# A hybrid attention and convolution block: gate and up computed by tokens, their product turned by VectorE and a trip through DRAM

## Chip, core and metric

The kernel runs on one core of one Trainium2 chip (trn2). The metric is the device time of one execution in microseconds, the median of three timed runs. The engines are named PE (TensorE matmul), PEld (TensorE weight load), DVE (VectorE), ACT (ScalarE), POOL (GpSimd) and SP (SyncE, which here only issues DMAs).

## What is computed

One block over 256 tokens of width 1024: a normalized input is projected, half of the width goes through attention with 8 heads, half through a causal convolution of 31 taps, both are projected back and added to the residual. Then comes the part that the change touches, a gated feed-forward layer of inner width 2816, and a last normalization:

```
h = h + mixed @ w_out[l]
u = rms_norm(h, ffn_norm_g[l])
h = h + (jax.nn.silu(u @ w_gate[l]) * (u @ w_up[l])) @ w_down[l]
...
return rms_norm(h, final_norm_g)
```

All inputs are float32.

## The kernel before

Every float32 operand of a large product is split into a high part (rounded to the fast float32r type, by ACT) and a low part (the rest, by DVE), and each product is three matmuls: high by high, high by low, low by high. The weights come in by SP's DMAs as raw tiles of 128 x 1024 (`load`, six buffers), `high` and `split` (L130 to L154) make `wh` and `wl` of them (nine buffers each), and `cut` (L156) takes columns out of them. Activations are kept turned, with the model width on the partitions: `xs` is the residual, `u2` holds the high and the low half of the normalized input, `uh` and `ul`, for all 256 tokens.

The phases ahead of the feed-forward layer follow a list of steps written out by hand (PROGRAM, L41). Its last lines hold the output projection (`f`), the lower halves of u (`g`), the squares for the norm (`hs`) and the first splits of the gate and up weights (`w.g0.0` and so on). Up to the product of group 0 all engines keep program order; then, at L627, ACT, DVE, POOL and SP are handed to the scheduler of the framework, and only PE stays in program order.

The feed-forward layer runs over 11 groups (FG) of 256 inner columns. For a group, `gate_up` (L552) has the weights as the held operand, 128 inner columns at a time (i), and streams u: one pass of 512 columns for the high weights (`uh` and `ul` side by side) and one of 256 for the low weights with `uh`, for 8 k, for gate and up (j). Gate and up come out with the inner width on the partitions, each in a PSUM bank of its own, four banks a group out of four. Group 0 goes by k in passes of 256 (`up_mm`, L548). `swiglu` (L572) adds the two halves of a bank (`both`: a copy on ACT, an addition on DVE), multiplies the gate by the per-token scale `rb2` (a broadcast that PE makes as `pb_h`, L616), takes Silu on ACT, multiplies by up on DVE and splits the product `ff` into `fh` and `fl`. These already have the form in which `down` (L588) holds them: 128 tokens by 128 inner rows, with `w_down` streamed in passes of 512, 24 passes a group, into four PSUM banks `pd` that are summed over all groups. On PE the order is gate-and-up of group g+1, then down of group g; the last two groups (HOLD, L620) are held back for the end. `h_rows` (L602) turns the residual for the end on PE, four transposes in each of the groups 1 to 4, into `ht`. At the end each half of the tokens gets its last products, the residual is added, squares are summed, and the scaled rows go out (L641 to L679).

Of the kernel before, what the change touches and what calls it, by code (L numbers as in the profile page):

```python
# [15 lines left out]
P = 128  # L16
S = 256
# [31 lines left out]
pv.0 mo.0 pv.1 mo.1 l.6 pv.2 mo.2 pv.3 mo.3 l.3 w.o1.1 ld.g0 w.o2.0 w.o2.1 ld.u0 o.0 o.1 l.7 w.o3.0 o.2 w.o3.1 ld.g1 l.4 l.5 w.g0.0 o.3 w.u0.0 o.4  # L49
f.0 f.1 g.0 f.2 g.1 f.3 g.2 f.4 g.3 f.5 g.4 f.6 g.5 f.7 g.6 g.7 w.g0.1 ld.u1 w.u0.1 ld.d0 hs.0 hs.1 hs.2 hs.3 hs.4 hs.5 hs.6 hs.7 w.g1.0 w.g1.1  # L50
# [9 lines left out]
def block_kernel(ctx, tc, xT, w_in, w_out, w_gate, w_up, w_down, pvec, gfin, relb, hot, out):  # L60
# [29 lines left out]

    steps = [t.split(".") for t in PROGRAM.split()]
# [452 lines left out]
    rb2 = w2.tile([P, S], F32, name="rb2")  # L544
    pd = [[bank(2 * t + n, f"pd{t}{n}") for n in range(2)] for t in range(2)]
    pf, acts = {}, {}

    def up_mm(g, i, j, k, start):  # L548
        mm3(pf[g][i][:, j * S : (j + 1) * S], "gu"[j] + str(g), k * S + i * P,
            uh[:, k], ul[:, k], start, k == KD - 1)  # L550

    def gate_up(g):  # L552
        pf[g] = []
        for i in range(2):
            pf[g].append([bank(next(spare), f"pf{2 * g + i}{j}") for j in range(2)])
            for j in range(2):
                o = pf[g][i][j]
                for k in range(KD):
                    wh, wl = cut("gu"[j] + str(g), k * S + i * P, P)
                    if k < KD - 1:  # L560
                        mm(o, wh, u2[:, k], start=k == 0, stop=False, skip_group_check=True)
                    mm(o[:, 0:S], wl, uh[:, k], start=False, stop=False, skip_group_check=True)
                    if k == KD - 1:
                        mm(o, wh, u2[:, k], start=False, stop=True, skip_group_check=True)

    def both(o, name):
        t = w2.tile([P, S], F32, name=name, tag="fb", bufs=2)
        act.copy(t, o[:, S : 2 * S])  # L568
        vec.tensor_add(t, o[:, 0:S], t)  # L569
        return t  # L570

    def swiglu(g):  # L572
        acts[g] = []
        for i in range(2):
            f = 2 * g + i
            gr = w2.tile([P, S], F32, name=f"fg{f}", tag="fg", bufs=2)
            vec.tensor_mul(gr, both(pf[g][i][0], f"fa{f}") if g else pf[g][i][:, 0:S], rb2)
            sg = w2.tile([P, S], F32, name=f"fs{f}", tag="fs", bufs=2)
            act.activation(sg, gr, AF.Silu)
            ff = w2.tile([P, S], F32, name=f"ff{f}", tag="ff", bufs=2)  # L580
            vec.tensor_mul(ff, sg, both(pf[g][i][1], f"fb{f}") if g else pf[g][i][:, S : 2 * S])
            fh = w2.tile([P, S], F32R, name=f"fh{f}", tag="fh", bufs=8)
            act.copy(fh, ff)
            fl = w2.tile([P, S], F32R, name=f"fl{f}", tag="fl", bufs=8)
            vec.tensor_sub(fl, ff, fh.bitcast(F32))  # L585
            acts[g].append((fh, fl))

    def down(g, i, t, lo, hi, o=None, start=None, stop=None):  # L588
        f = 2 * g + i
        tok = slice(t * P, (t + 1) * P)  # L590
        wh, wl = cut(f"d{g}", i * D + lo, hi - lo)
        fh, fl = (a[:, tok] for a in acts[g][i])
        if o is None:
            o = pd[t][lo // 512][:, lo % 512 : lo % 512 + hi - lo]
            start, stop = f == 0, f == NF - 1
# [12 lines left out]
    pf[0] = [bank(next(spare), f"pf{i}") for i in range(2)]  # L608
    for k in range(KD):
        for i in range(2):  # L610
            for j in range(2):
                up_mm(0, i, j, k, k == 0 and j == 0)
        if k == 5:
            rc2, dg2 = rstd(acch, D, RMS_EPS, "h", next(spare))
# [5 lines left out]
    HOLD = 2  # L620
    for g in range(FG):
        if 0 < g < FG - 1:
            split(f"g{g + 1}")
            split(f"u{g + 1}")
        swiglu(g)
        if g == 0:
            act, vec, pool, sync = nc.scalar, nc.vector, nc.gpsimd, nc.sync  # L627
        split(f"d{g}")
        if g + 1 < FG:
            gate_up(g + 1)  # L630
        if g < FG - HOLD:
            for i in range(2):
                for t in range(2):
                    for n in range(2):
                        down(g, i, t, n * 512, n * 512 + 512)
        if 1 <= g <= 4:
            h_rows((g - 1) // 2, (g - 1) % 2)


    held = [(g, i) for g in range(FG - HOLD, FG) for i in range(2)]  # L640
    for t in range(2):  # L641
# [8 lines left out]
        def square_rows(i, lo, hi):  # L650
            sq = w2.tile([P, 512], F32, name=f"fsq{t}{i}", tag="fsq", bufs=2)
            act.activation(sq[:, : hi - lo], ht[:, t, lo:hi], AF.Square, accum_out=ss[:, i : i + 1])
            vec.tensor_mul(hg[:, lo:hi], ht[:, t, lo:hi], gf[:, lo:hi])
# [9 lines left out]
        pe = bank(next(spare), f"pe{t}")  # L663
        for n, (g, i) in enumerate(held):
            down(g, i, t, 768, 1024, pe[:, 0:S], n == 0, n == len(held) - 1)
        ms = w2.tile([P, 2], F32, name=f"fms{t}")
        vec.tensor_add(ms[:, 0:1], ss[:, 0:1], ss[:, 1:2])
        vec.tensor_scalar(ms[:, 0:1], ms[:, 0:1], 1.0 / D, RMS_EPS, op0=ALU.mult, op1=ALU.add)
        add_rows(pe[:, 0:S], 768, 1024)
        square_rows(2, 768, 1024)  # L670
        vec.scalar_tensor_tensor(ms[:, 1:2], ss[:, 2:3], 1.0 / D, ms[:, 0:1], op0=ALU.mult, op1=ALU.add)
        rf = w2.tile([P, 1], F32, name=f"rf{t}")
        pool.tensor_tensor(rf, ms[:, 1:2], mhalf[:, 0:1], op=ALU.pow)
        vec.tensor_scalar(hg[:, 0:384], hg[:, 0:384], rf, None, op0=ALU.mult)
        nc.sync.dma_start(out[rows, 0:384], hg[:, 0:384])
        act.activation(hg[:, 384:704], hg[:, 384:704], AF.Copy, scale=rf)
        nc.scalar.dma_start(out[rows, 384:704], hg[:, 384:704])
        vec.tensor_scalar(hg[:, 704:1024], hg[:, 704:1024], rf, None, op0=ALU.mult)
        nc.sync.dma_start(out[rows, 704:1024], hg[:, 704:1024])  # L679
# [30 lines left out]

def _layout(x, mix_norm_g, w_in, rel_bias, conv_w, conv_b, conv_ln_g, conv_ln_b, w_out,
            ffn_norm_g, w_gate, w_up, w_down, final_norm_g):
    flat = lambda a: np.ascontiguousarray(a.reshape(P, -1))
    wi = _rows(w_in[0])
# [9 lines left out]
    pairs = lambda w: flat(_rows(w).reshape(P, KD, FG, S).transpose(0, 2, 1, 3))  # L724
# [33 lines left out]
```

## Time and profile before

| | |
|---|---|
| timed runs | 303.37, 303.93, 304.09 us; median 303.93 us |
| profiled execution | 304.98 us, of which the span from the first to the last instruction is 303.2 us |
| PE | 294.6 us busy, 1984 matmuls |
| DVE | 218.4 us busy |
| ACT | 166.6 us busy |
| DMA | 56.39 MB, mean 186 GB/s |
| feed-forward layer | from 109.4 us to the end |

The profile is of one execution. Busy time of PE is that of pipelined matmuls whose ends are modelled, so distances between the starts of matmuls say more than their durations. The chain of waits follows the work that ended last back to the start; a piece in it names the engine, the tile and the line.

### The profile page before, as it was taken

The page shows a single profiled execution, that of the slowest core. Times are in us where ns is not written, and L with a number is a line of the kernel's source. Part 1 is how long each engine was busy: PE and PEld are TensorE (multiplying, and loading weights), DVE is VectorE, ACT ScalarE, POOL GpSimd, SP SyncE. Part 2 cuts the span into 40 slices and gives each one's busy share as a digit, 9 for nine tenths or more (in the row PEclk, how much of TensorE's full clock was granted, in tenths as well). Part 3 has the DMA queues.
Part 4 walks back from the last instruction along what each step waited for, and adds up shares of the span by engine and source line. Part 5 has one row for each costly group of instructions (what it writes and reads, how often), then busy time and mean ns, then how long its engine had stood idle before and what let it go on. Part 6 is the DMA issues. An engine that isn't in the chain of part 4 may idle for free.

```text
span 303.2 us, 5198 instructions
## 1 busy us (share of the span) xinstructions
PE 294.6 (97%) x1984; PEld 258.6 (85%) x1984; DVE 218.4 (72%) x405; ACT 166.6 (55%) x300; POOL 8.2 (3%) x27
## 2 busy tenths in 40 slices
PE   8999999999999999999999999999999999999991
PEld 8998987897699999878888888888888888888891
DVE  3877999888987788898665749485665748383483
ACT  3875554364583678674645636374645546371242
POOL 4000000000000000000000000000000000000000
PEclk9999999999999999999999999999999999999998
DMA  6999879744418426988583846648283837300012
GB/s 186 351 387 325 260 181 287 312 138 142 128 23 301 142 105 200 298 283 282 189 271 83 273 136 216 199 129 272 83 277 85 277 129 240 109 0 2 0 54 85
DMA packets 18936, 56.39 MB, mean 186 GB/s; under 512 B 2221, under 2 KB 5061, under 8 KB 18912
## 3 DMA queue, kind: packets, MB, share of 16 engines
q1 hardware_dynamic: 18176, 54.99, 56.4%
q0 software_dynamic: 304, 0.74, 0.9%
q8 instruction: 15, 0.25, 0.3%
q10 hardware_dynamic: 432, 0.34, 0.3%
q14 instruction: 9, 0.07, 0.1%
HBM read 54.41 MB, written 1.65 MB: 185 GB/s over the span
## 4 chain that ended last, share of the span: by engine, by line
PE 74%; issue 11%; DMA 6%; DVE 3%; ACT 3%; SPq 1%; POOL 1%; POOLq 0%; DVEq 0%
PE pf L72 34%; PE pd L72 17%; PE pqk L72 7%; DMA raw_a<-in_w_in 4%; PE pv L72 4%; PE pc L72 4%; PE py L72 2%; DMA raw_u<-in_w_up 2%; PE ps L72 1%; SPq L83 1%; ACT wh_a L83 1%; PE pa L72 1%; PE pg L72 1%; PE pt L75 1%; PE po L72 1%
## 5 line engine op out<-in xcount | busy, mean ns | idle before, releaser
L72 PE MATMUL pf<-u,wh_u 128*128 128x512 f32 (+1 forms) x192 | 64.1, 375 | 0.6 <-DVE ff L83 0.6
L72 PE MATMUL pf<-u,wh_g 128*128 128x512 f32 (+1 forms) x192 | 64.6, 377 | 0.0
L72 PE MATMUL pf<-u,wl_g 128*128 128x256 f32 x176 | 46.1, 281 | 0.0
L72 PE MATMUL pf<-u,wl_u 128*128 128x256 f32 x176 | 46.1, 281 | 0.0
L72 PEld LDWEIGHTS pf<-u,wh_u 128*128 128x128 f32 x192 | 34.9, 188 | 6.0 <-DVE ff L83 0.9
L72 PEld LDWEIGHTS pf<-u,wh_g 128*128 128x128 f32 x192 | 34.9, 188 | 5.3
L72 PEld LDWEIGHTS pf<-u,wl_u 128*128 128x128 f32 x176 | 33.1, 188 | 1.7
L72 PEld LDWEIGHTS pf<-u,wl_g 128*128 128x128 f32 x176 | 33.2, 188 | 1.5
L154 DVE TENSOR_TENSOR wl_u<-raw_u,wh_u 128x1024 fp32r<-128x1024 f32 x18 | 21.9, 1224 | 16.7 <-ACT wh_u L144 16.7
L72 PE MATMUL pd<-wh_d,fh 128*128 128x512 f32 (+1 forms) x88 | 33.7, 383 | 0.0
L72 PE MATMUL pd<-wh_d,fl 128*128 128x512 f32 (+1 forms) x88 | 33.5, 381 | 0.0
L72 PE MATMUL pd<-wl_d,fh 128*128 128x512 f32 (+1 forms) x88 | 33.4, 379 | 0.0
L144 ACT CAST wh_u<-raw_u 128x1024 fp32r<-128x1024 f32 x18 | 18.9, 1048 | 17.9 <-PE pd L72 9.6
L154 DVE TENSOR_TENSOR wl_d<-raw_d,wh_d 128x1024 fp32r<-128x1024 f32 x22 | 26.8, 1216 | 0.7 <-ACT wh_d L144 0.6
L154 DVE TENSOR_TENSOR wl_g<-raw_g,wh_g 128x1024 fp32r<-128x1024 f32 x18 | 22.0, 1223 | 4.7 <-ACT wh_g L144 4.3
L144 ACT CAST wh_g<-raw_g 128x1024 fp32r<-128x1024 f32 x18 | 18.9, 1050 | 9.0 <-PE pd L72 7.9
L144 ACT CAST wh_d<-raw_d 128x1024 fp32r<-128x1024 f32 x22 | 22.7, 1052 | 1.4 <-PE pd L72 1.1
L72 PE MATMUL pqk<-u,wh_qk 128*128 128x256 f32 x128 | 23.1, 282 | 0.0
L569 DVE TENSOR_TENSOR fb<-pf,fb 128x256 f32<-128x256 f32 x20 | 8.4, 419 | 19.1 <-ACT fb L568 19.1
L72 PEld LDWEIGHTS pqk<-u,wh_qk 128*128 128x128 f32 x128 | 19.6, 188 | 0.4 <-issue 0.3
L72 PEld LDWEIGHTS pd<-wh_d,fl 128*128 128x128 f32 x88 | 16.5, 188 | 3.5 <-DVE fl L585 0.2
L72 PEld LDWEIGHTS pd<-wl_d,fh 128*128 128x128 f32 x88 | 16.6, 188 | 3.3
(165 smaller groups left out, 580.7 us busy)
## 6 DMA issues: line engine op xcount, KB each, us to landing
raw_g<-in_w_gate SPq DMA_DIRECT2D x22, 512.0 KB, 4.5
raw_u<-in_w_up SPq DMA_DIRECT2D x22, 512.0 KB, 4.3
raw_d<-in_w_down SPq DMA_DIRECT2D x22, 512.0 KB, 4.7
raw_qk<-in_w_in SPq DMA_DIRECT2D x8, 512.0 KB, 7.1
raw_o<-in_w_out SPq DMA_DIRECT2D x8, 512.0 KB, 4.1
ustk<-ud SPq DMA_DIRECT2D x8, 288.0 KB, 5.7
raw_a<-in_w_in SPq DMA_DIRECT2D x8, 256.0 KB, 4.8
raw_a<-in_w_in SPq DMA_DIRECT2D x4, 512.0 KB, 7.4
```

Source lines behind the costliest of these rows:

```text
L72: return tc.keep_in_program_order(nc.tensor.matmul(*args, **kw))
L75: return tc.keep_in_program_order(nc.tensor.transpose(o, i, ident))
L83: return lambda *a, **k: tc.keep_in_program_order(f(*a, **k))
L144: act.copy(wh[:, c], raw[:, c])
L154: vec.tensor_sub(wl[:, c], raw[:, c], wh[:, c].bitcast(F32))
L569: vec.tensor_add(t, o[:, 0:S], t)
```

## The change

Gate and up are computed with the tokens on the partitions: u is the held operand, 128 tokens at a time (t), and the weights are streamed 512 wide, 256 columns of gate beside 256 of up, in one tensor `w_gu`; 8 k, two token halves and three products make 48 passes of 512 a group, for group 0 too, in two PSUM banks. Silu reads PSUM with the per-token scale as a column, so `rb2`, `both` and the broadcast go. The product now has the tokens on the partitions and has to be turned before `down` can hold it. `send` turns 32 x 32 blocks on DVE, stores the tile to DRAM with POOL's queue in pieces of 64 elements, and loads it again in four DMAs; `land` splits it into `fh` and `fl` one group later, and down of group g follows gate-and-up of group g+2. The last group is turned by PE instead (`flip_ff`), and the last two groups' products stand at the end. The residual is turned in the same way (`h_turn` on DVE in groups 1 to 4, `h_rows` with six DMAs in group 4). The model width and the inner rows are permuted on the host to match the turned blocks. All engines keep program order throughout. In PROGRAM, `w.u0.0` and `w.g0.1` change places and `ld.d0` becomes `ld.g2`, and the load order has `w_down` two groups late.

```diff
@@ PROGRAM
-... w.g0.0 o.3 w.u0.0 o.4
-f.0 f.1 g.0 ... f.7 g.6 g.7 w.g0.1 ld.u1 w.u0.1 ld.d0 hs.0 ... w.g1.0 w.g1.1
+... w.g0.0 o.3 w.g0.1 o.4
+f.0 f.1 g.0 ... f.7 g.6 g.7 w.u0.0 ld.u1 w.u0.1 ld.g2 hs.0 ... w.g1.0 w.g1.1
...
-    for g in range(FG + 1):
+    for g in range(FG + 2):
         if g < FG:
-            order += [(w_gate, 2048 * g, f"g{g}"), (w_up, 2048 * g, f"u{g}")]
-        if g > 0:
-            order += [(w_down, 2048 * (g - 1), f"d{g - 1}")]
+            order += [(w_gu, 4096 * g, f"g{g}"), (w_gu, 4096 * g + 2048, f"u{g}")]
+        if g > 1:
+            order += [(w_down, 2048 * (g - 2), f"d{g - 2}")]
...
-    spare = iter((4, 5, 6, 7) + 200 * (6, 7, 4, 5))
+    spare = iter((4, 5, 6) + 200 * (7, 6, 4, 5))
...
+    def up_mm(g, t, k):
+        wh, wl = cut("gu"[k // 4] + str(g), k % 4 * 512, 512)
+        tok = slice(t * P, (t + 1) * P)
+        mm(pf[g][t], uh[:, k, tok], wh, start=k == 0, stop=False)
+        mm(pf[g][t], uh[:, k, tok], wl, start=False, stop=False)
+        mm(pf[g][t], ul[:, k, tok], wh, start=False, stop=k == KD - 1)
     def gate_up(g):
+        pf[g] = [bank(next(spare), f"pf{g}{t}") for t in range(2)]
+        for k in range(KD):
+            for t in range(2):
+                up_mm(g, t, k)
+    def swiglu(g):
+        for t in range(2):
+            sg = w2.tile([P, S], F32, name=f"fs{g}{t}", tag="fs", bufs=2)
+            act.activation(sg, pf[g][t][:, 0:S], AF.Silu, scale=rc2[:, t : t + 1])
+            ff[g, t] = w2.tile([P, S], F32, name=f"ff{g}{t}", tag="ff", bufs=4)
+            vec.tensor_mul(ff[g, t], sg, pf[g][t][:, S : 2 * S])
+    fd = [dram.tile([4, 2, P, 2 * 32], F32, name=f"fd{n}") for n in range(3)]
+    def send(g):
+        fv = w2.tile([P, 4, 2, 2 * 32], F32, name=f"fv{g}", tag="fv", bufs=2)
+        for t in range(2):
+            vec.transpose(fv[:, :, t], ff[g, t])
+        d = fd[g % 3]
+        pool.dma_start(d.rearrange("b t p c -> p (b t) c"), fv.rearrange("p b t c -> p (b t) c"))
+        fb[g] = w2.tile([P, 2, 4, 2, 32], F32, name=f"fb{g}", tag="fb", bufs=3)
+        for b in range(4):
+            pool.dma_start(fb[g][32 * b : 32 * b + 32].rearrange("p t a i s -> p (t a) (i s)"),
+                           d[b].rearrange("t (a j) c -> j (t a) c", a=4))
+    def land(g):
+        for t in range(2):
+            fh, fl = (a[:, t].rearrange("p i (a s) -> p i a s", a=4) for a in parts_of(g))
+            f = fb[g][:, t].rearrange("p a i s -> p i a s")
+            act.copy(fh, f)
+            vec.tensor_sub(fl, f, fh.bitcast(F32))
+    def flip_ff(g, t):
+        pt = bank(next(spare), f"pt{g}{t}")
         for i in range(2):
+            turn(pt[:, i * P : (i + 1) * P], ff[g, t][:, i * P : (i + 1) * P])
+        fh, fl = (a[:, t].rearrange("p i s -> p (i s)") for a in parts_of(g))
+        act.copy(fh, pt[:, 0:S])
+        vec.tensor_sub(fl, pt[:, 0:S], fh.bitcast(F32))
...
-    def h_rows(t, n):
-        pt = bank(next(spare), f"ph{t}{n}")
-        for i in range(4):
-            turn(pt[:, i * P : (i + 1) * P], xs[:, 4 * n + i, t * P : (t + 1) * P])
-        act.copy(ht[:, t, n * 512 : (n + 1) * 512], pt)
+    def h_turn(m):
+        tc.keep_in_program_order(vec.transpose(hb[:, :, m], xs[:, m].rearrange("p (b j) -> p b j", j=32)))
+    def h_rows():
+        for a in range(4):
+            tc.keep_in_program_order(pool.dma_start(bass.AP(tensor=hd.tensor, offset=hd.offset + a * S, ap=[[D, 32], [32 * D, KD], [1, S]]),
+                           hb[32 * a : 32 * a + 32].rearrange("p b m j -> p b (m j)")))
+        for t in range(2):
+            pool.dma_start(ht[:, t], hd[t * P : (t + 1) * P, :])
...
-    pb2 = wide(dg2, "h", next(spare))
-    act.copy(rb2, pb2[:, :S])
...
     for g in range(FG):
         swiglu(g)
-        if g == 0:
-            act, vec, pool, sync = nc.scalar, nc.vector, nc.gpsimd, nc.sync
-        split(f"d{g}")
-        if g + 1 < FG:
+        if g < FG - 1:
+            send(g)
             gate_up(g + 1)
-        if g < FG - HOLD:
+        if g > 0:
+            split(f"d{g - 1}")
+            land(g - 1)
+        if 0 < g < FG - 2:
             for i in range(2):
                 for t in range(2):
                     for n in range(2):
-                        down(g, i, t, n * 512, n * 512 + 512)
+                        down(g - 1, i, t, n * 512, n * 512 + 512)
+        if g < FG - 2:
+            split(f"g{g + 2}")
+            split(f"u{g + 2}")
         if 1 <= g <= 4:
-            h_rows((g - 1) // 2, (g - 1) % 2)
+            h_turn(2 * g - 2)
+            h_turn(2 * g - 1)
+        if g == 4:
+            h_rows()
+    split(f"d{FG - 1}")
+    for i in range(2):
+        for t in range(2):
+            for n in range(2):
+                down(FG - 3, i, t, n * 512, n * 512 + 512)
+        flip_ff(FG - 1, i)
...
+    a, b = FG - 2, FG - 1
     for t in range(2):
...
-        for g, i in held:
-            down(g, i, t, 0, 512)
+        last(a, t, 0, 512)
+        last(b, t, 0, 512)
         add_rows(pd[t][0], 0, 512)
         square_rows(0, 0, 512)
-        for g, i in held:
-            down(g, i, t, 512, 768)
+        gain_rows(0, 512)
+        last(a, t, 512, 1024)
         add_rows(pd[t][1], 512, 1024)
+        pe = [bank(next(spare), f"pe{t}{n}")[:, 0:S] for n in range(2)]
+        last(b, t, 512, 768, pe[0])
+        add_rows(pe[0], 512, 768)
         square_rows(1, 512, 768)
...
+        last(b, t, 768, 1024, pe[1])
```

## Rows read from the trace of the kernel before

**Rows 1.** The page: busy time of each engine, its share of the span, its instructions.
```profile
PE 294.6 (97%) x1984; PEld 258.6 (85%) x1984; DVE 218.4 (72%) x405; ACT 166.6 (55%) x300; POOL 8.2 (3%) x27
```

**Rows 2.** The chain of waits in order of time: start us, us, what.
```profile
133.78 5.48 PE pd L72 x24
139.25 11.18 PE pf L72 x64
...
155.91 0.44 PE ph L75 x4
...
285.39 2.81 PE pd L72 x12
```

**Rows 3.** Stretches: length; busy (count) of PE, PEld, DVE, ACT, POOL; clock, DMA share, GB/s.
```profile
167.51:184.60 17.09, 17.09 (x93) 14.69 (x93) 10.87 (x17) 9.37 (x15) 0.00 (x0) 1.00 0.58 184
...
218.78:235.43 16.65, 16.65 (x89) 14.30 (x89) 10.87 (x17) 8.89 (x14) 0.00 (x0) 1.00 0.59 191
```

**Rows 4.** Timeline of PE, value projection: start us, us, what; ten spacings apart.
```profile
69.94 0.40 PE L72 MATMUL pv<-wl_v,u 128*128 128x512 f32 x1
...
72.27 0.40 PE L72 MATMUL pv<-wh_v,u 128*128 128x512 f32 x1
```

**Rows 5.** Timeline of PE, a down group: its first, ninth and last pass.
```profile
150.27 0.40 PE L72 MATMUL pd<-wh_d,fh 128*128 128x512 f32 x1
...
152.12 0.39 PE L72 MATMUL pd<-wh_d,fl 128*128 128x512 f32 x1
...
155.52 0.39 PE L72 MATMUL pd<-wh_d,fl 128*128 128x512 f32 x1
```

**Rows 6.** Timeline of PE, group 0: first pass, 72 passes on, the broadcast, group 1.
```profile
109.39 0.40 PE L72 MATMUL pf<-u,wh_g 128*128 128x256 f32 x2
...
117.79 0.50 PE L72 MATMUL ps_h<-ones,acch 128*128 128x1 f32 x4
...
121.08 0.70 PE L72 MATMUL pb_h<-dg_h,ones 128*128 128x256 f32 x2
...
121.85 0.28 PE L72 MATMUL pf<-u,wl_g 128*128 128x256 f32 x1
```

**Rows 7.** Timeline of PE, group 1: in brackets the idle time before, and its releaser.
```profile
129.76 0.40 PE L72 MATMUL pf<-u,wh_g 128*128 128x512 f32 x1
130.72 0.50 PE L72 MATMUL pf<-u,wh_u 128*128 128x512 f32 x1 [0.57 <-DVE ff L83]
131.06 0.28 PE L72 MATMUL pf<-u,wl_u 128*128 128x256 f32 x1
```

**Rows 8.** Timeline of PE, transposes of the residual and the passes behind them.
```profile
155.75 0.60 PE L75 MATMUL ph<-ident,xs 128*128 128x128 f32 x4
...
156.41 0.28 PE L72 MATMUL pf<-u,wl_g 128*128 128x256 f32 x1
```

**Rows 9.** Timeline of PE, the end: twelve passes of 256, then 512.
```profile
289.45 0.28 PE L72 MATMUL pe<-wh_d,fh 128*128 128x256 f32 x1
...
290.89 0.40 PE L72 MATMUL pd<-wh_d,fh 128*128 128x512 f32 x1
```

**Rows 10.** Groups of instructions: what, count | busy us, mean ns | idle before, releaser.
```profile
L154 DVE TENSOR_TENSOR wl_d<-raw_d,wh_d 128x1024 fp32r<-128x1024 f32 x22 | 26.8, 1216 | 0.7 <-ACT wh_d L144 0.6
L144 ACT CAST wh_d<-raw_d 128x1024 fp32r<-128x1024 f32 x22 | 22.7, 1052 | 1.4 <-PE pd L72 1.1 <-ACT wh_d L144 0.3
L581 DVE TENSOR_TENSOR ff<-fs,fb 128x256 f32<-128x256 f32 x20 | 8.4, 421 | 0.3
```

**Rows 11.** POOL's issue (timeline), the page's DMA issue row, its row of a queue.
```profile
31.90 0.62 POOL L83 DMA_DIRECT2D ud<-upad  x1 [5.84 <-DVE upad L83]
...
ud<-upad POOLq DMA_DIRECT2D x2, 290.0 KB, 4.3
...
q10 hardware_dynamic: 432, 0.34, 0.3%
```

More of the change, by code (lines that the diff above doesn't have):

```diff
@@ L59, in block_kernel @@
 @with_exitstack
-def block_kernel(ctx, tc, xT, w_in, w_out, w_gate, w_up, w_down, pvec, gfin, relb, hot, out):
+def block_kernel(ctx, tc, xT, w_in, w_out, w_gu, w_down, pvec, gfin, relb, hot, out):
     nc = tc.nc
@@ L538, in block_kernel @@
     ph1.close()
-    spare = iter((4, 5, 6, 7) + 200 * (6, 7, 4, 5))
+    spare = iter((4, 5, 6) + 200 * (7, 6, 4, 5))
     w2 = ctx.enter_context(tc.tile_pool(name="w2", bufs=1))
     gf = w2.tile([P, D], F32, name="gf")
-    rb2 = w2.tile([P, S], F32, name="rb2")
     pd = [[bank(2 * t + n, f"pd{t}{n}") for n in range(2)] for t in range(2)]
[L546 to L550, printed above, removed]
@@ L552, in gate_up @@
-    def gate_up(g):
-        pf[g] = []
-        for i in range(2):
[L555 to L586, printed above, removed]
+    pf, ff, acts = {}, {}, {}
@@ new lines, in parts_of @@
+    def parts_of(g):
+        if g not in acts:
+            acts[g] = [w2.tile([P, 2, 2, P], F32R, name=f"{n}{g}", tag=n, bufs=3) for n in ("fh", "fl")]
+        return acts[g]
+    def land(g):
[6 more added lines that the diff above has]
+        pt = bank(next(spare), f"pt{g}{t}")
+        for i in range(2):
+            turn(pt[:, i * P : (i + 1) * P], ff[g, t][:, i * P : (i + 1) * P])
+        fh, fl = (a[:, t].rearrange("p i s -> p (i s)") for a in parts_of(g))
+        act.copy(fh, pt[:, 0:S])
+        vec.tensor_sub(fl, pt[:, 0:S], fh.bitcast(F32))
@@ L600, in block_kernel @@
     ht = w2.tile([P, 2, D], F32, name="ht")
-    def h_rows(t, n):
-        pt = bank(next(spare), f"ph{t}{n}")
-        for i in range(4):
-            turn(pt[:, i * P : (i + 1) * P], xs[:, 4 * n + i, t * P : (t + 1) * P])
-        act.copy(ht[:, t, n * 512 : (n + 1) * 512], pt)
-    pf[0] = [bank(next(spare), f"pf{i}") for i in range(2)]
+    hb = w2.tile([P, KD, KD, 32], F32, name="hb")
+    hd = dram.tile([S, D], F32, name="hd")
+    def h_turn(m):
[6 more added lines that the diff above has]
+            pool.dma_start(ht[:, t], hd[t * P : (t + 1) * P, :])
+    pf[0] = [bank(next(spare), f"pf0{t}") for t in range(2)]
     for k in range(KD):
-        for i in range(2):
-            for j in range(2):
-                up_mm(0, i, j, k, k == 0 and j == 0)
+        for t in range(2):
+            up_mm(0, t, k)
         if k == 5:
-            rc2, dg2 = rstd(acch, D, RMS_EPS, "h", next(spare))
+            rc2, _ = rstd(acch, D, RMS_EPS, "h", next(spare))
             split("u1")
-    pb2 = wide(dg2, "h", next(spare))
-    act.copy(rb2, pb2[:, :S])
     nc.sync.dma_start(gf, bass.AP(tensor=gfin.tensor, offset=gfin.offset, ap=[[0, P], [1, D]]))
-    HOLD = 2
     for g in range(FG):
-        if 0 < g < FG - 1:
-            split(f"g{g + 1}")
-            split(f"u{g + 1}")
         swiglu(g)
-        if g == 0:
-            act, vec, pool, sync = nc.scalar, nc.vector, nc.gpsimd, nc.sync
-        split(f"d{g}")
-        if g + 1 < FG:
+        if g < FG - 1:
+            send(g)
             gate_up(g + 1)
-        if g < FG - HOLD:
+        if g > 0:
+            split(f"d{g - 1}")
+            land(g - 1)
+        if 0 < g < FG - 2:
             for i in range(2):
@@ L634, in block_kernel, with last @@
                     for n in range(2):
-                        down(g, i, t, n * 512, n * 512 + 512)
+                        down(g - 1, i, t, n * 512, n * 512 + 512)
+        if g < FG - 2:
+            split(f"g{g + 2}")
+            split(f"u{g + 2}")
         if 1 <= g <= 4:
-            h_rows((g - 1) // 2, (g - 1) % 2)
-    held = [(g, i) for g in range(FG - HOLD, FG) for i in range(2)]
+            h_turn(2 * g - 2)
[4 more added lines that the diff above has]
+    for i in range(2):
+        for t in range(2):
+            for n in range(2):
+                down(FG - 3, i, t, n * 512, n * 512 + 512)
+        flip_ff(FG - 1, i)
+    def last(g, t, lo, hi, *o):
+        for i in range(2):
+            down(g, i, t, lo, hi, *((o[0], i == 0, i == 1) if o else ()))
+    a, b = FG - 2, FG - 1
     for t in range(2):
```

46 lines of the change are left out of this document (25 added, 21 removed).

## Prediction

> **What bounds the kernel now.** I read the line of busy times first: PE is busy for 294.6 of 303.2 us, DVE for 218.4, ACT for 166.6 [rows 1]. A busy PE alone proves little, so the chain of waits comes next: from 133.8 us to 285.4 us it holds nothing but PE pieces, in a period of one gate-and-up group (11.18 us, 64 matmuls), one down group (5.48 us, 24 matmuls) and, four times, 0.44 us of transposes of the residual [rows 2]. The table of stretches says that the other engines keep up: in one period of 17.09 us DVE works 10.87 us, ACT 9.37 us, POOL nothing, the 16 DMA engines are 0.58 busy, and the granted clock is 1.00 [rows 3]. So the end is set by what PE is given to do in 109 to 296 us and by the few places where it waits there. Work taken from DVE and ACT is worth nothing by itself; work or waits taken from PE count in full. The profiled execution took 304.98 us for a span of 303.2 us, the median of the timed runs is 303.93 us. I make the sum as a difference against the profiled execution and subtract it from the median too.
>
> **The change part by part.**
>
> *Gate and up, groups 1 to 10.* Before, a group is 32 passes of 512 columns (weights held, both halves of u streamed) and 32 of 256. After, u is held and the weights are streamed: 8 k by 2 token halves by 3 products, 48 passes of 512. The columns are the same, 24,576. Only the spacing of passes decides. Before it is 11.18 us a group [rows 2], which is 349 ns for a pair of 512 and 256. What will 48 passes of 512 cost? Two rows bound it. In the value projection (pv), where also u is held and a 512-wide weight is streamed, three products per bank in the same loop over k and tokens, ten spacings take 2.33 us, so 233 ns [rows 4]. In the down groups, where the product is held and a 512-wide weight is streamed, the first eight spacings take 1.85 us (231 ns), the fifteen after them 3.40 us (227 ns) [rows 5]. At 233 ns a group is 11.18 us: nothing gained. At 227 ns it is 10.88 us: 0.30 us gained. I take 233 ns, because pv is the same form with the same held tile; over ten groups that is 0, with -3.0 us as the other end.
>
> *Group 0.* Before it is 96 passes of 256 at 117 ns (72 of them in 8.40 us) [rows 6], 11.2 us; after, 48 of 512, 11.18 us at 233 ns: 0, or -0.3 us at 227 ns. Its second half of the weights is split where g0's and u0's second halves were, and is wanted later (k from 4 on), so nothing waits. The row scale is now applied in the Silu, per token, so the broadcast of it (pb_h) goes: from its start to the second pass after it are 0.77 us where one pass takes 0.24 [rows 6]: -0.53 us.
>
> *The wait in group 1.* PE stands 0.57 us for a PSUM bank that the product of group 0 still holds, and starts slowly behind it: 0.96 and 0.34 us instead of 0.235 and 0.23 [rows 7]. After, a group takes two banks and four rotate, so group g+1 writes banks that group g-1 left a whole group earlier: -0.84 us. Next late there would be the weights of group 2, which are split behind the Silu of group 0; they are first wanted a whole group (11.2 us) later, and their four casts and four subtractions take 4.2 and 4.9 us [rows 10].
>
> *Residual.* The 16 transposes on PE go: 0.66 us from the first to the second pass of the next group, instead of 0.24, so 0.42 us, four times: -1.70 us [rows 8]. In their place VectorE turns eight 128x256 tiles, two a group. No such operation is in the trace; below it cannot be under nothing, above I take twice the 0.42 us of a 128x256 product [rows 10], 1.7 us a group, which lies in the 6 us that DVE is idle in a period [rows 3]. Six DMAs on POOL's queue carry it through DRAM in group 4; it is wanted after group 10.
>
> *The product's way.* ACT and DVE lose four copies, four additions and two multiplications a group and gain at most two turned tiles. Then POOL's queue issues one store and four loads a group, each of 256-byte pieces, 2,048 in all. The loads wait in POOL's queue for the store to land; nothing but the next group's store is behind them, save the residual's DMAs once. Issuing: two DMAs of 290 KB took up to 0.62 us of POOL and 4.3 us to land [rows 11]. Lower end: 5 issues of 0.62 us and 4.3 us, 7.4 us of POOL a group; upper end: issue time grows with the pieces (1,024 against 128), 5 us for the store and 5 us for the loads, 14.3 us. Both are under the period of 16.65 us; I take the lower, since the rows are nearer. DMA time: a packet of mean 0.79 KB takes 34 ns of an engine (0.3% of 16 spans over 432 packets) [rows 11], so at most 2,048 x 34 / 16 = 4.4 us a group, which brings the share from 0.59 to 0.85. The way's price is then nothing, hidden by two groups: ACT reads the returned tile some 17 us after it was sent (a period of 16.65 us, and the next Silu and two casts ahead of the copy), and PE wants it some 12 us after that (what is left of a down group, and a gate-and-up group of 11.18 us, less the splits). If it comes late, the copy waits at ACT's head (the kernel after keeps program order on every engine throughout), behind it the casts of the weights of group g+2, and PE for these.
>
> [...] No row here has 256-byte stores. [...]
>
> *The end.* The last group is turned by PE, four transposes at about 0.105 us: +0.42 us. Six passes of 256 and six of 256 (pairs at 1.44 us for 12 [rows 9]) become six of 512 in each token half, 1.38 us: -0.1 us in all. The order of the last sums and multiplications changes, but the last add, square, power and scale still follow the last pass one by one: 0, give or take 0.15 us. New is that ACT and DVE split d9 and d10 only behind the Silu of group 10. Counted from the end of the last gate-and-up pass, DVE has two products, four splits of 1.22 us, and four lower parts of 0.42 us [rows 10], about 7.4 us with the first wait; PE has 24 passes, two pairs of transposes and six passes (7.3 us), and the third pass after that wants the last of these. That is 0.4 us to spare, so nothing is lost, but not by much.
>
> *Sum.* -0.53 - 0.84 - 1.70 + 0.42 - 0.10 = -2.75 us, with 0 for the wide passes: 302.2 us against the profiled execution, 301.2 us against the median. The nine down groups count as before, 5.48 us; at 233 ns throughout they would be 1.1 us dearer together, at 227 ns 0.4 us cheaper.
>
> **The rivals.**
>
> *The wide passes do pay.* Once they run without 256-wide passes between them, all settle at the 227 ns that the down groups reach after eight passes [rows 5]. For it: the slow first eight of each down group follow the mixed stream, and a run of 48 gives time to settle. Against it: pv never settles in its twelve. Price: -3.0 - 0.3 - 0.4 us more, -6.4 us: 297.5 us.
>
> *The end gives it back.* If the splits of d9 and d10 and the last lower parts come 2 us later than counted (the casts waiting on a transfer, or the flips late in ACT's order), PE stands these 2 us in front of the last products, and the end follows: 303.2 us, within what can't be told apart. It decides from 0.4 us on.
>
> *The DRAM trip becomes the bound (slower).* If POOL and the DMA engines need more than a period, 16.65 us, for one group's trip, each of the nine groups sent falls behind by the excess, and after some 12 us of lead are used up the copy on ACT, the weight splits behind it and PE wait for it. At 20 us a trip: 9 x 3.4 - 12, about +18 us: 320 us. It needs issues of 3 us or more instead of the 0.6 us in the row, or DMA share at its limit. The rows speak against it, and no row shows 256-byte pieces.
>
> **How the numbers follow.** Wide passes buy nothing, the removed pieces count: 0.54, time 301.2 us. Wide passes at 227 ns: 0.26, 297.5 us. Given back at the end: 0.10, 303.2 us. DRAM trip: 0.10, 320 us and around. About 0.3% (0.9 us) is what a measurement of this kernel can tell from no change. So faster 0.80, same 0.10, slower 0.10. The range takes in the first three and leaves out the last: 297.0 us (the second case with the measured spread) to 303.4 us.
>
> **What would show it.** Right: no wait of PE in the group loop; no ph and pb_h; the first pass of group 1 without a stand; pf at 48 passes in 11.2 us by the chain, or in 10.9 us for the first rival; loads of the returned product landed before ACT asks. Wrong: ACT's copy of the returned product idle on a DMA, with PE waiting on wh or wl behind it; PE idle on fl or wl_d after the last transposes; a spacing above 235 ns in pf, for each nanosecond of which 528 passes cost 0.5 us.

## The result, and the profile after

The kernel after takes 301.89 us (median of 12 runs, 301.11 to 303.60), the kernel before beside it 304.08 us: ratio of the mean times 0.9922, 95% interval 0.9903 to 0.9940, so 2.4 us less (1.8 to 2.9). 301.2 us was predicted, with a difference of -2.75 us. The profiled execution of after took 301.12 us, with a span of 299.3 us.

The page of after, in the columns of [rows 1], then its rows of the POOL queue, and of the trip's issues (KB of each, median us from issue to landing):

```profile
PE 291.7 (97%) x1750; PEld 246.0 (82%) x1750; DVE 203.5 (68%) x373; ACT 149.8 (50%) x255; POOL 44.2 (15%) x83
...
q0 software_dynamic: 2992, 8.08, 9.6%
...
fd<-fv POOLq DMA_DIRECT2D x10, 256.0 KB, 4.1
fb<-fd POOLq DMA_DIRECT2D x40, 64.0 KB, 5.7
```

DVE lost 15 us of work and ACT 17 us, POOL gained 36 us; PE still has 97% of the span. The chain of waits (start us, us, what), from group 0 on, answers [rows 2]:

```profile
108.44 8.39 PE pf L72 x36
116.82 0.34 PE ps_h L72 x4
117.16 25.32 PE pf L72 x108
142.48 5.46 PE pd L72 x24
147.94 11.20 PE pf L72 x48
...
285.70 1.45 PE pe L72 x12
```

From the first gate-and-up pass to the last products PE follows PE: no broadcast pb_h, no wait in group 1, no ph between pd and pf. A gate-and-up group of 48 wide passes takes 11.20 us where 64 mixed ones took 11.18 [rows 2]: 233 ns a pass, the rate of the value projection [rows 4]. The down groups take 5.45 us where they took 5.48 [rows 2].

To compare kernels without the part ahead of the feed-forward block, I take from each timeline of PE the start of the first gate-and-up pass and the start of the first pe pass of the second token half, near the end (`pe` is the bank of the last sums). Up to there both kernels have streamed the same columns of that half. The end points, in before and in after:

```profile
295.07 0.28 PE L72 MATMUL pe<-wh_d,fh 128*128 128x256 f32 x1
...
291.08 0.28 PE L72 MATMUL pe<-wh_d,fh 128*128 128x256 f32 x1
```

Before: 109.39 [rows 6] to 295.07, 185.68 us. After: 108.27 (the chain gives this piece a later start) to 291.08, 182.81 us, so **2.87 us less**. The spans differ by 3.9 us, but 1.1 us of that lies ahead of 108.27. That start lay between 108.13 and 109.66 us in all kernels of this study, also in those that do not differ ahead of it, so one profiled execution cannot put it down to the change.

### The profile page after: what moved, and what is told of

Same layout as the page of the kernel before. It is cut to its first block, busy times and chain, and to the rows that moved or that the text cites. A ratio compares the mean times of both kernels' runs of the same rounds, so it can differ in the third digit from the quotient of the medians.

```text
span 299.3 us, 4767 instructions
## 1 busy us (share of the span) xinstructions
PE 291.7 (97%) x1750; PEld 246.0 (82%) x1750; DVE 203.5 (68%) x373; ACT 149.8 (50%) x255; POOL 44.2 (15%) x83
## 2 busy tenths in 40 slices
DMA packets 21624, 63.73 MB, mean 213 GB/s; under 512 B 3117, under 2 KB 5957, under 8 KB 21600
## 3 DMA queue, kind: packets, MB, share of 16 engines
q0 software_dynamic: 2992, 8.08, 9.6%
## 4 chain that ended last, share of the span: by engine, by line
PE 96%; issue 2%; DVE 0%; POOL 0%; POOLq 0%; ACT 0%; DVEq 0%; ACTq 0%
PE pf L72 41%; PE pd L72 18%; PE py L72 8%; PE pqk L72 8%; PE pa L72 4%; PE pv L72 4%; PE pg L72 4%; PE pc L72 4%; PE wm L72 1%; PE ps L72 1%; PE pt L75 1%; PE po L72 1%; PE pe L72 0%; PE pz L72 0%; POOLq L805 0%
## 5 line engine op out<-in xcount | busy, mean ns | idle before, releaser
L72 PE MATMUL pf<-wh_u,u 128*128 128x512 f32 x176 | 57.4, 396 | 0.0
L72 PE MATMUL pf<-wh_g,u 128*128 128x512 f32 x176 | 57.1, 395 | 0.0
L72 PEld LDWEIGHTS pf<-wh_u,u 128*128 128x128 f32 x176 | 33.1, 188 | 7.9
L72 PEld LDWEIGHTS pf<-wh_g,u 128*128 128x128 f32 x176 | 33.1, 188 | 7.8
L72 PE MATMUL pf<-wl_u,u 128*128 128x512 f32 x88 | 34.8, 396 | 0.0
L72 PE MATMUL pf<-wl_g,u 128*128 128x512 f32 x88 | 34.8, 395 | 0.0
L72 PE MATMUL pd<-wh_d,fh 128*128 128x512 f32 x84 | 32.9, 392 | 0.0
L72 PE MATMUL pd<-wh_d,fl 128*128 128x512 f32 x84 | 32.8, 390 | 0.0
L72 PE MATMUL pd<-wl_d,fh 128*128 128x512 f32 x84 | 32.7, 389 | 0.0
L83 POOL DMA_DIRECT2D fb<-fd x40 | 23.2, 586 | 47.7 <-DMA fd<-fv 13.9
L83 ACT CAST wh_u<-raw_u 128x1024 fp32r<-128x1024 f32 x22 | 22.7, 1051 | 14.3 <-PE pf L72 10.9
```

The costliest lines, as they stand in the source:

```text
L72: return tc.keep_in_program_order(nc.tensor.matmul(*args, **kw))
L83: return lambda *a, **k: tc.keep_in_program_order(f(*a, **k))
```

## The experiments

The theory: PE's own work sets the time, and the gain is the PE work that was removed. The rivals: the wide passes, the relief of DVE and ACT, or a hidden price of the DRAM trip. "PE stretch" below is the measure of the last paragraph, read in each run.

| kernel | ratio to before (95%) | PE stretch, us | against |
|---|---|---|---|
| before | 1 | 185.68 | |
| after | 0.9922 (0.9903 to 0.9940) | 182.81 | before -2.87 |
| e1, narrow passes | 0.9988 (0.9966 to 1.0009) | 184.95 | after +2.14 |
| e2, one bank at a time | 0.9908 (0.9890 to 0.9926) | 182.81 | after 0.00 |
| e3, copies of u | 0.9828 (0.9807 to 0.9850) | 180.16 | after -2.65 |
| e4, product turned on PE | 1.0082 (1.0053 to 1.0112) | 187.30 | after +4.49 |
| e5, residual turned on PE | 1.0135 (1.0103 to 1.0166) | 188.90 | after +6.09 |
| e5b, the same, copy later | 0.9970 (0.9952 to 0.9988) | 184.51 | after +1.70 |
| e6, before with new residual | 0.9957 (0.9937 to 0.9977) | 183.82 | before -1.86 |
| e7, one group late | 1.0610 (1.0584 to 1.0636) | 203.69 | after +20.88 |
| e8, u moved by 32 bytes | 0.9818 (0.9792 to 0.9845) | 179.28 | after -3.53 |
| e9, weights moved by 32 bytes | 0.9833 (0.9806 to 0.9861) | 179.29 | after -3.52 |
| e10, before, u moved | 1.0039 (1.0023 to 1.0055) | 186.03 | before +0.35 |
| e11, u at two places | 0.9800 (0.9774 to 0.9826) | 179.29 | after -3.52 |

### Are the wide passes a part of the gain? (e1)

```
-        mm(pf[g][t], uh[:, k, tok], wh, start=k == 0, stop=False)
+        for j in range(2):
+            c = slice(j * S, (j + 1) * S)
+            mm(pf[g][t][:, c], uh[:, k, tok], wh[:, c], ...)
```

(and so for the two other products)

> The changed kernel, but each 512-wide weight pass of gate and up is cut into two passes of 256 with the same held tile, 96 passes a group instead of 48. Theory (the wide passes bought nothing, because PE's time goes by columns): 72 passes of 256 took 8.40 us in group 0 of the kernel before, so 96 take 11.20 us against 11.19 us for 48 wide ones; the time stays at the changed kernel's, about 2.4 us under the kernel before (ratio 0.992). Rival (the wide passes are a source of the gain): a group gets longer by 0.2 us or more, and the run loses 2 us or more, which brings it to the time of the kernel before (ratio 0.999 or above).

The chain of e1, one group:

```profile
148.29 11.36 PE pf L72 x96
```

118.3 ns a pass, not the 116.7 of group 0 before [rows 6]: there the weights were held and u was moved, here u is held. That is 0.16 us a group, and the down groups behind it take 5.50 instead of 5.45 us; together 2.1 us. The group grew by a little less than the rival's 0.2 us, but the time went where the rival said (2.1 us; ratio 0.9988). So in this form a 512-wide pass (233 ns) is cheaper than two of 256 (twice 118.3 ns). That does not make it a source of the gain over before, whose mixed group took 11.18 us: the removed pieces are, and cutting the passes would have eaten most of it.

### Why 233 ns and not 227? (e2, e3, e8, e9)

e2 runs one token half after the other:

```
-        for k in range(KD):
-            for t in range(2):
+        for t in range(2):
+            for k in range(KD):
                 up_mm(g, t, k)
```

> The changed kernel, but groups 1 to 10 of gate and up run all 24 passes of one token half before the other, so PE stays on one PSUM bank for 24 passes instead of three. It tests why these passes come every 233 ns and those of the down groups every 227 ns. If the change of bank every three passes costs it: 227 ns, a group of 10.9 us instead of 11.19 us, and 10 x 0.3 = 3 us less than the changed kernel (ratio to the kernel before about 0.982). If the held tile u is the cause (or anything else that this order leaves alone): spacing 233 ns, the time stays at ratio 0.992. Small in either case: the second token half of the product comes 5.6 us after the first, so the first Silu can start earlier; no gain is expected of that since PE does not wait for it.

Nothing moved: groups of 11.19 us, the same stretch to a hundredth. The change of bank is not the cause.

e3 holds copies of u:

```
+    u3 = [w2.tile([P, KD, 2, P], F32R, name=f"u3{n}") for n in "hl"]
+    for k in range(KD):
+        pool.tensor_copy(u3[0][:, k]..., uh[:, k]...)
+        pool.tensor_copy(u3[1][:, k]..., ul[:, k]...)
...
+        a, b = (uh..., ul...) if g < 2 else (u3[0][:, k, t], u3[1][:, k, t])
```

> The changed kernel, with the upper and lower part of u copied by GpSimd to two tiles of the later pool, and groups 2 to 10 of gate and up holding the copies; groups 0 and 1 hold the tile as before. If the place of the held tile (its address, or the two parts side by side) makes the 233 ns: groups 2 to 10 at 227 ns, 10.9 us each, while groups 0 and 1 stay at 11.19 us, and about 9 x 0.3 = 2.7 us less than the changed kernel (ratio about 0.983). If not: 233 ns in all groups and ratio 0.992. The 16 copies take GpSimd some microseconds ahead of the first trip of the product, which may come late by that much; PE has 12 us of lead there, so no wait is expected.

The chain of e3 (the first 36 passes of group 0, then group 3):

```profile
109.29 8.39 PE pf L72 x36
...
148.75 10.88 PE pf L72 x48
```

Same instructions, same data, another address: 10.88 us for 48 passes, 226.7 ns. Group 0 keeps its 8.39 us for 36. Two things differ between u and its copies: the region, and where they begin. By the allocation in the compiled programs u begins 128 bytes beyond a multiple of 512 in each partition, and the split weights, the split product and the copies all begin 96 beyond one. e8 moves u alone by 32 bytes against the weights, e9 moves everything behind u by 32 bytes:

```
+    pad = [const.tile([P, 8], F32, name="pad0")]          # e8
     u2 = const.tile([P, KD, 2, S], F32R, name="u2")
+    pad.append(const.tile([P, 8], F32, name="pad1"))      # e8
+    pad = [const.tile([P, 8], F32, name="pad0")]          # e9, instead
```

> The changed kernel, with the tile u moved by 32 bytes in each partition (8 spare columns ahead of it and 8 behind it, so that all later tiles move by 64). In the changed kernel u begins at a multiple of 64 bytes, and the split weights and the split product begin at 32 beyond one; the copies of u that came every 227 ns also began at 32 beyond one. If it is this that counts, that held and moving tile begin alike within 64 bytes: 227 ns in all groups from 0 on, and in the value projection too, 11 x 0.3 + 0.3 = 3.6 us less than the changed kernel (ratio to the kernel before about 0.980). If it is the region (u at 24 KB, its copies at 167 KB and above): 233 ns and ratio 0.992.

> The changed kernel, with 8 spare columns behind u, so that u stays and every tile behind it, the split weights and the split product among them, moves by 32 bytes to a multiple of 64. If held and moving tile have only to begin alike within 64 bytes: 227 ns in all groups, 3.6 us less than the changed kernel (ratio 0.980). If the held tile alone decides, and has to begin 32 bytes beyond a multiple of 64: 233 ns in the gate-and-up groups and now also in the down groups, 9 x 0.14 = 1.3 us more than the changed kernel (ratio 0.996). If the region decides: 233 and 227 ns as in the changed kernel, ratio 0.992.

The chain of after in the attention part (query-key and value projection), to compare with:

```profile
30.12 8.45 PE pqk L72 x72
...
55.83 2.80 PE pv L72 x12
```

The chain of e8, the same and from group 0 on:

```profile
30.15 8.64 PE pqk L72 x72
...
56.23 2.75 PE pv L72 x12
...
108.79 8.18 PE pf L72 x36
...
147.38 10.88 PE pf L72 x48
```

The chain of e9, one group:

```profile
148.40 10.88 PE pf L72 x48
```

In both, 227 ns from group 0 on, with 3.5 us less than after and ratios of 0.982 and 0.983. The region is not it, nor one particular start of the held tile: in e9 u has not moved at all. What the two share, with e3, is that held and moved tile begin at the same place modulo 512 bytes; in after they are 32 bytes apart. The runs know only these two cases, so whether 64, 128 or 512 bytes is the measure stays open, and why it matters too. One row goes the other way: the query-key projection, 256-wide with the weights held, is slower in e8 and in e9, 8.64 instead of 8.45 us for 72 passes (120 against 117 ns).

### Does it hold for the kernel before? (e10)

The edit is that of e8, in the kernel before.

> The kernel before, unchanged but for u moved by 32 bytes as in the run on the changed kernel, so that u and the split weights begin alike within 64 bytes. Here the weights are held in gate and up and u is streamed. If likeness of the two is what counts, whichever is held: a gate-and-up group of 32 x 768 columns at 226.7 ns for 512, 10.88 us instead of 11.18 us, and with group 0 and the value projection about 3.5 us less than the kernel before (ratio 0.988). If only the held tile of the narrow form (u held) is concerned: nothing but the value projection, ratio 0.999.

It does not. The chain of e10, group 0 and group 2:

```profile
109.82 8.64 PE pf L72 x72
...
139.17 11.28 PE pf L72 x64
```

Group 0 takes 8.64 us where it took 8.40 [rows 6], and the groups 11.28 us where they took 11.18: 3 ns more for each pair of a 512-wide and a 256-wide pass, as much as the 256-wide alone lost in group 0. The kernel is 0.4% slower. The PE stretch grows by only 0.35 us, though these rows alone make some 1.2 us (0.24 in group 0, 0.1 in each of groups 2 to 10): PE does not wait in group 1 of this run, where it stood 0.57 us before [rows 7], and a down group takes 5.45 us instead of 5.48. So likeness is not a general good: with the weights held and u moved it cost 3 ns on a 256-wide pass and gave nothing on the 512-wide ones between them; with u held it saved 6.5 ns on a 512-wide pass. The kernel before stood at the better of its two places. Only the change to held tokens and wide passes made the other place worth 3.5 us.

### The turn of the product on PE instead of the DRAM trip (e4)

```
-        if g < FG - 1:
-            send(g)
+        if g > 0:
+            flip_ff(g - 1)        # four transposes, one copy and subtraction a half
+        if g < FG - 1:
             gate_up(g + 1)
         if g > 0:
             split(f"d{g - 1}")
-            land(g - 1)
...
```

> The changed kernel, with the product of groups 0 to 9 turned by PE (four transposes a group ahead of the next gate-and-up group, one copy and one subtraction from PSUM) in place of the turn on VectorE and the DRAM trip. Theory (the trip costs nothing, and PE's work alone sets the time): four transposes cost PE 0.42 us, as the residual's did before, so 10 x 0.42 = 4.2 us more than the changed kernel, 1.8 us slower than the kernel before (ratio 1.006). Rival (the trip has a hidden price, in DMA share or in ACT's and DVE's waits): the time rises by clearly less than 4 us, or falls.

The chain of e4, the transposes of one group and the group behind them:

```profile
148.30 0.44 PE pt L75 x4
148.74 11.20 PE pf L72 x48
```

4.49 us more in the PE stretch: about 0.35 us for four transposes, and by the timeline the 48 passes behind them take 11.28 instead of 11.19 us. That is 0.44 us a group, ten times. The ratio, 1.6% above that of after (4.9 us), agrees within its interval. Theory had 4.2 us. No price of the trip shows: taking it away gave nothing back.

### The residual (e5, e5b, e6)

```
+    def h_rows(t, n):
+        pt = bank(next(spare), f"ph{t}{n}")
+        for i in range(4):
+            turn(pt[:, i * P : (i + 1) * P], xs[:, 4 * n + i, t * P : (t + 1) * P])
+        act.copy(ht[:, t]..., pt...)        # e5; in e5b issued behind the next swiglu(g)
...
-            h_turn(2 * g - 2)
-            h_turn(2 * g - 1)
+            h_rows((g - 1) // 2, (g - 1) % 2)
```

> The changed kernel, with the residual turned by PE again, four transposes behind the down passes of four groups. Theory: 4 x 0.42 = 1.7 us more than the changed kernel (ratio to the kernel before 0.998). Rival (the residual's turn was hidden anyway, or its DMAs cost as much): the changed kernel's time, ratio 0.992.

6.1 us instead of 1.7. The chain of e5 around the first of its four places, and ACT's timeline there:

```profile
148.76 0.45 PE ph L75 x4
...
149.72 0.49 ACT fs L83
...
150.23 0.43 DVE ff L83
...
150.71 1.43 PE pf L72 x5
```

```profile
149.24 0.59 ACT L83 COPY ht<-ph 128x512 f32<-128x512 f32 x1 [7.78 <-PE ph L75]
149.72 0.84 ACT L83 ACTIVATE fs<-pf,rc_h 128x256 f32<-128x256 f32 x2
```

ACT stood 7.78 us at the copy, which waits for PE's transposes behind the down group, and the Silu of the next group stood behind it in ACT's order. PE then waited for the bank that this Silu's product frees, and went on late: 1.5 us a place with the transposes, four times. The row of these waits of PE (total, times, longest):

```profile
PE pf L72 <- DVE ff L83: 3.2, 4, 0.8
```

That is my edit's fault and no price of the transposes, which e5b shows:

> As the last run with the residual on PE, but ACT's copy of the turned residual is issued behind the next group's Silu instead of ahead of it. In that run PE waited four times 0.8 us for a PSUM bank whose product stood behind this copy. Theory: without that wait only the transposes are left, four times 0.42 to 0.45 us, so 1.7 to 1.8 us more than the changed kernel (ratio to the kernel before 0.998). If the turn on PE costs more than its own time for another reason: a ratio of 1.005 or above again.

1.70 us by the PE stretch, ratio 0.997. From the other side:

> The kernel before with one part of the change alone: the residual turned by VectorE and two DRAM passes instead of 16 transposes on PE (with the order of features in memory that this needs). Theory: 4 x 0.42 = 1.7 us less than the kernel before, ratio 0.994. Rival (it was hidden, or the DMAs cost as much, where ACT and DVE are still as loaded as before): ratio 1.000 or above.

1.86 us less by the PE stretch: 1.70 and a somewhat shorter wait in group 1. The interval of the ratio, 0.9937 to 0.9977, includes the 0.994 of the theory. In the chain of e6 a gate-and-up group follows the down group directly, without transposes between them:

```profile
149.43 5.48 PE pd L72 x24
154.91 11.18 PE pf L72 x64
```

### One group late instead of two (e7)

```
-            order += [(w_down, 2048 * (g - 2), f"d{g - 2}")]
+            order += [(w_down, 2048 * (g - 1), f"d{g - 1}")]
...
-            split(f"d{g - 1}")
-            land(g - 1)
+        split(f"d{g}")
...
+            land(g)
...
-                        down(g - 1, i, t, n * 512, n * 512 + 512)
+                        down(g, i, t, n * 512, n * 512 + 512)
...
```

(the splits of the weights of group g+2 move ahead of `land`, too)

> The changed kernel, with each product's down passes one group late instead of two: the trip of group g has to be done when gate and up of group g+1 end. From the end of a gate-and-up group on, the trace of the changed kernel has the store issued after 2.1 us, the loads landed after about 14.5 us and the copy and lower part done after about 15.6 us. With a down group and a gate-and-up group between, PE wants it after 16.65 us: about 1 us to spare, so no wait in the later groups. Only the first trip, which ended late at 138.8 us, has no down group ahead of it: PE would want it at about 130.8 us and wait 8.5 us. Theory: 8 to 9 us more than the changed kernel, all of it in front of the first down group, ratio to the kernel before 1.020. Rival (the trip has no such spare time, or the copies pull it late): a wait of PE in each of the groups, 2 us or more each, ratio 1.05 or above.

20.9 us, not 8 to 9: the ratio, 1.061, is the rival's, but there is no wait in each group, as the rival had it. PE's waits have two places. First the row of waits for PE (total, times, longest), then POOL's timeline in group 4, where the residual's DMAs are:

```profile
PE pd L72 <- ACT fh L83: 16.7, 2, 8.6
```

```profile
199.71 2.32 POOL L83 DMA_DIRECT2D fb<-fd  x4 [3.64 <-DMA fd<-fv]
210.28 2.32 POOL L83 DMA_DIRECT2D hd<-hb  x4 [8.25 <-DVE hb L83]
218.66 1.13 POOL L83 DMA_DIRECT2D ht<-hd  x2 [6.05 <-issue]
219.77 0.92 POOL L83 DMA_DIRECT2D fd<-fv  x1
230.01 2.33 POOL L83 DMA_DIRECT2D fb<-fd  x4 [9.32 <-issue]
```

The first wait (8.6 us) is the first trip, as expected. That its size agrees is in part luck: the last lower part of that trip ends at 137.4 us in after, not at 138.8, and the trip was longer here, 15.0 us from the store's issue to the last landing where after has 11.8. The second (8.1 us) is the trip behind the residual's six DMAs: its loads are issued 10.2 us after its store, where 4.5 us is usual. I had left out that this queue is shared. (In e5b, where the residual stays out of this queue, the loads of no trip behind the first are issued more than 5.0 us after their store.) Of the other 4.2 us, 3.9 are the clock. Stretches of e7 (columns of [rows 3]), each wait and the down group behind it:

```profile
129.30:140.70 11.40, 2.85 (x13) 1.96 (x11) 1.88 (x2) 0.41 (x3) 2.33 (x4) 0.76 0.73 260
140.70:148.60 7.90, 7.84 (x25) 6.31 (x26) 6.75 (x10) 4.94 (x8) 2.18 (x4) 0.70 0.50 164
...
226.36:234.60 8.24, 0.17 (x2) 0.01 (x1) 0.02 (x1) 0.46 (x2) 2.33 (x4) 0.77 0.30 107
234.60:241.60 7.00, 7.00 (x25) 5.69 (x26) 6.73 (x10) 4.88 (x7) 1.12 (x2) 0.78 0.44 136
```

Behind these two waits of 8.6 and 8.1 us the granted clock of the next stretch is 0.70 and 0.78 on the mean, and the down groups take 7.8 and 7.0 us instead of 5.45. By the timeline the passes behind the first wait come every 0.43 us up to 145.2 us and every 0.23 us from 145.6 us on. In the six other groups of the loop PE does not wait, as the 1 us to spare had said.

### Both places of u (e11)

```
-    u2 = const.tile([P, KD, 2, S], F32R, name="u2")
+    ub = const.tile([P, KD * 2 * S + 8], F32R, name="u2")
+    u2, u4 = (ub[:, n : n + KD * 2 * S]... for n in (8, 0))   # u4: feed-forward part
```

> The changed kernel, with u in a tile longer by 8 columns, used at two places 32 bytes apart: up to the attention u begins unlike the weights within 64 bytes (as in the changed kernel), in the feed-forward part it begins like them. The runs with u or the weights moved showed both sides: with like beginnings the 512-wide passes came every 226.7 instead of 233.2 ns, but the 256-wide passes of the query-key projection took 23.53 us instead of 23.04 us for 192 (120 instead of 117 ns). If both follow from the beginnings alone: query-key projection 23.04 us, value projection 11.59 us as in the changed kernel, gate-and-up groups 10.88 us, 3.3 us less in the feed-forward part than the changed kernel, and a time 0.3 to 0.8 us under the run in which u was moved throughout (ratio to the kernel before about 0.980; that last difference is too small for the times and is read from the rows). If the length of the tile, or what u was used for before, matters: another spacing in one of the two parts.

The chain of e11:

```profile
31.06 8.45 PE pqk L72 x72
...
56.78 2.80 PE pv L72 x12
...
148.08 10.88 PE pf L72 x48
```

Each part has the spacing of its place: 8.45 us and 2.80 us as in after, 10.88 us as in e8. With 298.63 us (ratio 0.980) it beats both kernels; against e8 (0.982) the times cannot tell.

## Why the prediction came out

The steps in the PE stretch, predicted and read from the timelines of both kernels:

| step | predicted | read |
|---|---|---|
| pb_h and the wait in group 1 | -1.37 | -1.38 (groups 0 and 1: 24.23 us in before; 22.85 in after) |
| residual's transposes | -1.70 | -1.70 (e5b) |
| last group turned on PE | +0.42 | +0.39 (the ninth down group with its four transposes, 5.86 us, against 5.48) |
| held products, wider passes | -0.10 | -0.12 |
| wide passes, groups 2 to 10 | 0 | +0.15 (11.194 against 11.177 us) |
| eight down groups | 0 | -0.20 (5.453 against 5.478 us) |
| sum | -2.75 | -2.86 |

The residual's term is shown by runs, from both sides (e5b, e6). The terms of group 0 and 1 are read from the timelines alone: no run puts the broadcast back, and none tells whether the wait went because a group takes two banks instead of four or because ACT and DVE have less to do ahead of the product that frees the bank. Nor does a run relieve ACT and DVE alone; but that wait, 0.57 us [rows 7], is the only one of PE in this stretch of before, so their relief can have given no more than this term holds.

**The wide passes.** 233 ns was taken from the value projection, the same form with the same held tile, and it came so; the other end, 227 ns, was the rival of 297.5 us. That rival named the wrong cause: not a run of like passes that settles, for 48 in a row do not settle, but where u begins. With u moved by 32 bytes its price came nearly whole, 3.5 of 3.7 us. The step was right for this kernel by the choice of the nearest row, not by a known reason: the value projection holds the same tile, so the place of u was in that row unseen.

**The turn on DVE.** Bounds were 0 to 0.84 us; the row of groups for after has 0.42, that of a 128x256 product [rows 10], half of the upper end:

```profile
L83 DVE STREAM_TRANSPOSE fv<-ff 128x256 f32<-128x256 f32 x20 | 7.6, 420 | 0.0
```

**The trip.** It was to be hidden, and was: PE waits nowhere in the group loop of after. POOL's timeline in after, a usual group and the one behind the residual:

```profile
161.08 0.90 POOL L83 DMA_DIRECT2D fd<-fv  x1 [8.09 <-DVE fv L83]
165.47 2.31 POOL L83 DMA_DIRECT2D fb<-fd  x4 [3.50 <-issue]
...
197.15 0.93 POOL L83 DMA_DIRECT2D fd<-fv  x1
209.31 2.33 POOL L83 DMA_DIRECT2D fb<-fd  x4 [11.24 <-ACT fs L83]
```

The usual trip shown holds POOL's queue for 6.7 us: 0.9 us of issue, 3.5 us until the store has landed, 2.3 us of issue for four loads. Bounds were 7.4 and 14.3 us and the lower was taken; the issue hardly grew with the pieces (0.90 us for 1,024, 0.585 for 256, where 0.62 stood for 128 [rows 11]). The last of its loads landed 14.0 us after the store's issue, and ACT read it 17.0 us after that issue, as the prediction had it. Two trips were late for ACT, by its timeline:

```profile
136.23 0.71 ACT L83 CAST fh<-fb 128x256 fp32r<-128x256 f32 x2 [2.56 <-DMA fb<-fd]
...
213.34 0.71 ACT L83 CAST fh<-fb 128x256 fp32r<-128x256 f32 x2 [1.87 <-DMA fb<-fd]
```

These are the first trip and the one behind the residual's DMAs, whose loads were issued 12.2 us after the store instead of 4.4. PE wants the first at 142.5 us by the chain (6 us after ACT read it, where the prediction had 12 for every trip), and the second a gate-and-up group later than ACT, so it did not notice; with one group less (e7) it waits at just these two. The prediction named the residual's DMAs in this queue, "once", but priced them at nothing without saying what covers them.

**DMA.** The queue of the trip took 9.6% of 16 spans, 28.7 us for ten trips, the residual and the padded conv rows, so under 2.9 us a group where 4.4 was the bound; a usual period has a share of 0.72 (predicted up to 0.85):

```profile
158.97:175.62 16.65, 16.65 (x74) 13.52 (x73) 9.75 (x14) 7.45 (x10) 3.21 (x5) 1.00 0.72 221
```

2,992 packets carried 8.08 MB, 2.7 KB each. The page counts 3,117 packets under 512 B, where before had 2,221: 896 more, for 20,480 pieces of 256 bytes that ten trips send, and the queue's 2,992 packets are far fewer than these pieces, so the pieces are not packets of their own. The third rival did not come about: it needed more than 16.65 us of POOL or DMA for a trip; a usual trip held POOL's queue for 6.7 us, and the DMA time was under 2.9 us a group. (The rival counts nine trips; ten are sent.)

**The end.** 0.4 us to spare were counted, against the wrong lower part. Timelines of DVE, PEld and PE in after:

```profile
282.36 0.75 DVE L83 TENSOR_TENSOR fl<-pt,fh 128x256 fp32r<-128x256 f32 x2
...
283.05 0.19 PEld L72 LDWEIGHTS pd<-wh_d,fl 128*128 128x128 f32 x1
283.27 0.39 PE L72 MATMUL pd<-wh_d,fl 128*128 128x512 f32 x1
```

The row of DVE holds two lower parts of 0.41 us, one for each token half. The pass at 283.27 works on the first half and needs the first of them, which ends at 282.77: 0.28 us before the load of this pass starts, 0.50 before the pass. The last one, which the prediction had in its place, ends at 283.11, after that load began, and is wanted only in the second half of the tokens, after 286.97. So the step held, though not as it was counted, and the second rival (the end gives 2 us back) did not come about, by some tenths of a microsecond.

## What to carry to other kernels

Where one engine is busy through the whole stretch, price a change by that engine's own instructions, pass by pass, and ask of all the rest only whether it is late: 15 us less of DVE and 17 us less of ACT gave nothing beyond, at most, the end of one wait; 16 transposes, a broadcast and that wait gave nearly all. The trip through DRAM cost PE nothing here while its whole length (two landings, two issues, and whatever else stood in its queue; 17.0 us up to ACT's read in the usual trip) fitted the lead of two groups, and one group less of lead cost 21 us, in two places, a fifth of it by the clock. Before believing a pass's spacing, move the held tile by 32 bytes: here that was worth 3.5 us.

## What had not been expected

- The spacing of passes depended on whether held and moved tile begin alike (modulo 512 bytes) or 32 bytes apart; no run has another distance. With tokens held, 512 wide: 226.7 ns begun alike, 233.2 ns 32 bytes apart. With weights held, 256 wide: 120 ns alike, 117 ns apart. The reason is open.
- 256-wide passes with u held, 32 bytes apart, came every 118.3 ns (e1), so two cost 3.4 ns more than a 512-wide one.
- POOL's issue of a DMA grew little with its pieces: 0.90 us for 1,024, 0.585 us for 256.
- The two waits of 8 us cost PE 2.4 and 1.5 us more in the down group behind them, at a granted clock of 0.70 and 0.78.
